# Paired score banks and raised product runs in a hybrid mixer step on one core

## The chip, the cores and the metric

The kernel runs on one core of a Trainium2 chip. The metric is the device time of one execution in microseconds (us), smaller is better. The core has TensorE (PE in the profile; PEld are its weight loads), VectorE (DVE), ScalarE (ACT), GpSimd (POOL) and SyncE (SP, which here issues most of the DMAs). Products of TensorE are written to PSUM, which has eight banks; a bank holds 128 partitions of 512 float32 numbers.

## The reference

One layer of a mixer with three branches over the same input, for 128 context tokens and 512 latent tokens (a grid of 8 rows of 64), width 1024:

```
h     = rmsnorm(x, g_pre) * (1 + scale) + shift      # shift, scale, gate = silu(c) @ w_ada + b_ada
proj  = h @ w_in                                     # 3840 columns
A  8 heads x 64: latent queries see a window of 16 columns of the grid and 256 cached context
   keys in one softmax, with a learned bias; context tokens see the context only
B  4 heads x 64: gated linear recurrence in both directions (HGRN2), state 64 x 64 a head
C  2-D Fourier transform over positions and channels, then a 256 x 256 matrix
out   = concat(A * silu(ga), B * silu(gr), C * silu(gf)) @ w_out
y     = x + gate * rmsnorm(out, g_post)
```

The outputs are y, the context's keys and values, and the final states of the recurrence.

## The kernel before

**Precision and tiling.** Most products run in float32r with both operands split into a high and a low part, and three products are added for each (`mm3`: high x high, low of the input x high of the weights, and the other way round). All 640 tokens stand side by side as columns. The 3840 columns of `w_in` are handled as blocks of 128; a block's result for 320 tokens (half a block) is one bank, filled by 8 x 3 products with 320 columns each (`block`, lines 297 to 312). The weights of a block arrive as 512 KB, are cast to the high part on ScalarE and subtracted on VectorE.

**Streams.** The work is written as generators, which `Order` (lines 39 to 68) merges by estimated times: `start_stream` (modulation vectors, transposed input), `zf_stream` (first two gate blocks, four banks at once), `fill` (all other blocks, in the order of `FILL`), two recurrences, the four attentions of two heads each, the gate vectors of the output, the Fourier branch, and the two halves of the output projection (`out_first`, `out_second`). The merged program order isn't the final one. The kernel is built with `schedule_with_timeline_sim`: a planner keeps a simulated time line, and whenever an engine comes free there, gives it the first instruction in program order whose operands and buffers are ready in the simulation. On the chip every engine then works through its own list in that order. `tc.issue_after` and manual dependencies without a semaphore tie instructions in this planning.

**PSUM.** `PB` (line 105) gives one bank of one of two kinds: tag `b` with five banks, tag `f` with three. `f` holds the half blocks and other sums of the filling streams, three of the four sums of the first gate blocks (line 206) and one of the two tiles in `by_token` (line 343). `b` holds the rest: the transposed input (`px`, `pm`), scores, levels, transposed softmax, weighted values, the recurrence's products and the first output sums. A bank is free again when its last reader is done.

**Products with half the rows.** A head is 64 wide, so two heads share the 128 partitions, head 1 in the upper half of the array's rows, head 0 in the lower. Where a product sums over a head's channels, it takes 64 rows. Three places make such runs and write head 1 and head 0 in turn:
- `level` (lines 431 to 450): for each of seven levels and two head pairs, products `t` x `t` for five units of 128 tokens, four units in one pair of banks and the fifth in another. A float32 product shows as two instructions, so a level has twenty. VectorE merges them under a mask (line 450), ScalarE copies the first level.
- `scores` (lines 641 to 647) from `softmax_latent` (line 669): two calls, six products on the cached keys (`kc`) and six on the latent keys (`tks`), both with the queries `tqs`, into a pair of banks.
- `scores` from `softmax_context` (line 651): six products of 128 columns.

`follow` (line 115) makes each product of such a run come behind the one before it. It doesn't keep other products from between them.

`mod_cols` (lines 192 to 198) makes eight products of 32 output rows each, four side by side in four quarters of the array's columns, sixteen instructions in the profile; `start_stream` calls it twice for each of eight steps, `gate_vectors` once for each of eight blocks. There is no such chain in it.

**Around the softmax.** `softmax_latent` reads the scores on VectorE (maxima, lines 675 and 676) and on ScalarE (the exponentials, lines 679 and 680), then `transposes` (line 705) turns the result with four transposes a head into a bank of `b`, which two casts on ScalarE and two subtractions on VectorE (lines 127 and 128, `pT`) empty. Scores of a tile are issued behind the transposes of the tile two before it (`AHEAD`).

Of the kernel before, what the change touches and what calls it, by code (L numbers as in the profile page):

```python
# [17 lines left out]
P = 128  # L18
# [7 lines left out]
TOKENS = ("ir",)  # L26
WB = {"raw": 2, "hi": 3, "lo": 3, "t": 18, "pe": 2, "o": 4, "cf": 3, "pb": 5, "pf": 3, "s": 8, "m": 4, "row": 2, "tbl": 1, "pT": 8, "vs": 2, "kc": 4}
RAW = ["vs", "pT", "pT", "pT"] * 4
# [43 lines left out]
def mixer_kernel(ctx: ExitStack, tc: tile.TileContext, A, O):  # L72
# [31 lines left out]

    def PB(tag="b"):
        return ps.tile([P, 512], F32, tag=tag, name=nm("pb"), bufs=WB["p" + tag])

# [6 lines left out]

    def follow(chain, ins):

        if chain:
            tc.add_manual_dep(ins, chain[-1].name, mybir.DependencyInfo(mybir.DependencyClass.NoSync,
                                                                        mybir.DependencyReason.DATA), reason="turns")
        chain.append(ins)  # L120
# [70 lines left out]

    def mod_cols(out, w):

        t = od.now
        for k in range(KT):
            o = out[32 * (k % 4):32 * (k % 4) + 32, :]
            mm(o, csil[:, k, :], w[:, k, :], start=(k < 4), stop=(k >= 4))
        od.now = t + 0.45
# [5 lines left out]
    def xcols(i, k):  # L204
        return (xa[i] if k < 5 else xb[i])[:, k % 5 * P:k % 5 * P + P]
    zf_w, zf_acc = [], [[PB("f"), PB("f")], [PB("f"), PB()]]

# [34 lines left out]
    def start_stream():  # L242
        load_x()
        raws, zraw = [], []

        def loads(k):
            for u in range(2):
                raws.append(load_raw(A["wss"][2 * k + u], RAW[2 * k + u]))
            if k < 2:
                zraw.append(load_raw(A["win"][k], "raw"))  # L250

        for k in range(EARLY):
            loads(k)
        scale_x()
        od.now = 11.0
        for k in range(KT):
            if k + EARLY < KT:
                loads(k + EARLY)
            row = sp.tile([P, 256], F32, tag="AC", name=nm("row"), bufs=2)
            pm = PB()  # L260
            for u in range(2):
                mod_cols(pm[:, u * P:(u + 1) * P], raws[2 * k + u])
            yield 0
            ve.tensor_copy(row, pm[:, 0:256])
            yield LAT["row"]

            for u in range(2):
                tr(pm[:, u * P:(u + 1) * P], row[:, u * P:(u + 1) * P])
            pt = S(4)
            ve.reduce_sum(pt, pm[:, 0:256].rearrange("p (u g r) -> p u r g", u=2, r=32)[:, :, 0:2, :], axis=AX.X)  # L270
            ve.tensor_scalar(G[:, k, :], pt[:, 0:2], bss[:, k, 0:1], 1.0, op0=ALU.add, op1=ALU.add)
            ve.tensor_scalar_mul(G[:, k, :], G[:, k, :], gpre[:, k:k + 1])  # L272
            ve.tensor_scalar_add(shift[:, k, :], pt[:, 2:4], bss[:, k, 1:2])
            modulated(k, pm)
            if k < 2:
                zf_w.append(split_w(zraw[k]))
            if k == 1:
                od.set("zw", 0.0)
            yield max(0.0, 13.5 + 2.7 * (k + 1) - od.now)
# [17 lines left out]
    def block(name, use, lo_eng=ve):  # L297

        w = load_w(A["win"][BLOCKS.index(name)], lo_eng)
        for u in range(2):  # L300
            acc = PB("bf"[u] if name == "zb0" else "f")[:, 0:320]
            for k in range(KT):
                if name == "zb0" and u == 0 and f"h{k}" not in od.events:
                    yield f"h{k}"
                mm3(acc, w, k, u, k == 0, k == KT - 1)
                if k % 2 and k < KT - 1:
                    yield 0
            use(acc, u)
            if u == 1:
                od.set(f"block{nb[0]}", 0.0)  # L310
                nb[0] += 1
            yield 0
# [28 lines left out]
    def by_token(src):  # L341

        pt = PB(), PB("f")
        for i in range(5):
            tr(pt[i // 4][:, i % 4 * P:i % 4 * P + P], src[:, i * P:(i + 1) * P])
        return [(slice(4 * j, 4 + j), pt[j][:, 0:(4, 1)[j] * P].rearrange("p (i e) -> p i e", e=P)) for j in range(2)]

    def token_blocks(name, use, tokens, lo_eng=ve):
# [4 lines left out]
        for i0, n in ((0, 2), (2, 2), (4, 1)):  # L353
            acc = PB("f")[:, 0:256 * n].rearrange("p (i e) -> p i e", e=256)
            for i in range(n):
# [58 lines left out]
    def recurrence(p):  # L414
# [16 lines left out]
        def level(KB, QB, li):  # L431
# [3 lines left out]
            for i0, i1 in ((0, 4), (4, 5)):  # L435
                pa = [PB(), PB()]
                t, chain = od.now, []
                for i in range(i0, i1):
                    for hh in (1, 0):
                        ins = mm(pa[hh][:, (i - i0) * P:(i - i0 + 1) * P], KB[RS[hh], i * P:(i + 1) * P],  # L440
                                 QB[RS[hh], i * P:(i + 1) * P])
                        follow(chain, ins)
                od.now = 0.5 * (t + od.now)
# [84 lines left out]

        po = PB(), PB()
        for i in range(5):  # L530
# [106 lines left out]
    def attention(p):  # L637
# [3 lines left out]
        def scores(outs, qt, keys, chain):  # L641

            cols, t = slice(qt * P, (qt + 1) * P), od.now
            for n, (a, b) in enumerate(((0, 0), (0, 1), (1, 0))):
                for hh in (1, 0):
                    follow(chain, mm(outs[hh], qs[a][RS[hh], cols], keys(b)[RS[hh]], start=(n == 0), stop=(n == 2)))
            od.now = 0.5 * (t + od.now)
# [3 lines left out]
        def softmax_context():  # L651
            pss, pes = [PB(), PB()], []
            scores([t[:, 0:P] for t in pss], 0, lambda b: ks[b][:, 0:P], [])
# [15 lines left out]
        def softmax_latent(qt):  # L669
            pss, pes, chain = [PB(), PB()], [], []  # L670
            scores([t[:, 256:512] for t in pss], 1 + qt, lambda b: kcs[b], chain)
# [109 lines left out]
    def fourier_blocks():  # L781
# [7 lines left out]
        for g in range(2):  # L789
            WCS[g] = [T(512, dt=F32R) for _ in range(2)]  # L790
            pw = PB("f")
            for a in range(2):
# [5 lines left out]
    def fourier():  # L798
        Z = [None] * 5
        for i in range(5):  # L800
            pz = PB("f")
            for g in range(2):
# [24 lines left out]
        for u in range(2):  # L827
            pf = PB("f"), PB("f")
            for j in (4, 1, 3, 2, 0):
# [14 lines left out]
    def gate_vectors():  # L844
        selr = cp.tile([P, 2, P], F32R, tag="selr", name="selr")
        gp.tensor_copy(selr, sel)
        for q in range(8):
# [13 lines left out]
            if q % 2 == 0:  # L861
                rows = [sp.tile([P, 256], F32R, tag="AC", name=nm("row"), bufs=2) for _ in range(2)]
            pm, es = PB("f"), slice(q % 2 * P, q % 2 * P + P)
            mod_cols(pm[:, 0:P], w)
            split(pm[:, 0:P], *[t[:, es] for t in rows])
            if q % 2 == 0:
                continue
            yield 1.0
            pg, cs = PB("f"), slice(q % 4 * P - P, q % 4 * P + P)
            for d in range(2):  # L870
# [24 lines left out]
    def out_first():  # L895
# [7 lines left out]
        units = out_units(0, (3,))  # L903
        banks = [PB() for _ in range(4)]
        for n, k in enumerate(kord):
# [3 lines left out]
            for i in range(4):  # L909
                out_mm(banks[i], units[k], i, k, n == 0, n == KT - 1)  # L910
                yield 0
        banks.append(PB("b" if WB["pb"] > 4 else "f"))
        for n, k in enumerate(kord):
# [5 lines left out]
    def out_second():  # L919
# [5 lines left out]
        for i in range(5):  # L925
# [16 lines left out]
            for c in range(0, 512, w):  # L942
                po, cs = PB("f"), slice(c, c + w)
                pieces.append((po, 1, cs))
# [184 lines left out]
```

## Time and profile before

| | |
|---|---|
| runs timed | 3: 436.21, 436.61, 437.71 us |
| median | 436.61 us |
| the profiled execution | 437.11 us |
| its span, first to last instruction | 435.3 us |
| mean granted TensorE clock | 0.996 |
| DMA | 47.62 MB, mean 109 GB/s |

The profile is of one execution. Its span leaves out 1.8 us of that execution's time, ahead of the first and behind the last instruction. In rows of the timeline the columns are: start (us from the span's start), duration, engine, source line, operation, tile written and tiles read, active rows x columns of the array, shape, count of instructions merged into the row, and in brackets the engine's idle time before it with what ended it. Line 113 is the helper `mm` and line 124 the helper `tr`, so products are told apart by tiles: `pb<-hT,hi` and `pb<-hT,lo` are half blocks, `pb<-t,t` with 64 rows are levels, `pb<-kc,tqs` and `pb<-tks,tqs` scores, `pb<-raw,csil` the gate vectors, `pb<-ident,pe` the transposed softmax. A product's duration includes time in the pipeline that it shares with its neighbours; the distance between starts is what it takes from the stream. In rows of the windows the columns are: stretch, its length, then busy time and count for PE, PEld, DVE, ACT and POOL, granted clock, mean busy share of the DMA engines, GB/s.

### The profile page before, as it was taken

The page shows a single profiled execution, that of the slowest core. Times are in us where ns is not written, and L with a number is a line of the kernel's source. Part 1 is how long each engine was busy: PE and PEld are TensorE (multiplying, and loading weights), DVE is VectorE, ACT ScalarE, POOL GpSimd, SP SyncE. Part 2 cuts the span into 40 slices and gives each one's busy share as a digit, 9 for nine tenths or more (in the row PEclk, how much of TensorE's full clock was granted, in tenths as well). Part 3 has the DMA queues.
Part 4 walks back from the last instruction along what each step waited for, and adds up shares of the span by engine and source line. Part 5 has one row for each costly group of instructions (what it writes and reads, how often), then busy time and mean ns, then how long its engine had stood idle before and what let it go on. Part 6 is the DMA issues. An engine that isn't in the chain of part 4 may idle for free.

```text
span 435.3 us, 8309 instructions
## 1 busy us (share of the span) xinstructions
PE 411.3 (94%) x3176; PEld 372.7 (86%) x3176; DVE 303.5 (70%) x866; ACT 205.8 (47%) x546; POOL 7.4 (2%) x23
## 2 busy tenths in 40 slices
PE   0699999999998999999999999999999999999994
PEld 0488899999988998999899889889898988988884
DVE  2775479999986866885597658885768928670174
ACT  6434467565341526654444444753556643350161
POOL 2000000000020100000000000000000000000000
PEclk9999999999999999999999999999999999999998
DMA  7996153211302021122021413245134302481023
GB/s 236 412 407 229 49 158 114 74 45 50 88 20 76 10 62 48 56 97 74 32 68 60 145 50 104 98 147 163 51 119 150 96 0 66 140 291 48 0 105 139
DMA packets 19528, 47.62 MB, mean 109 GB/s; under 512 B 3184, under 2 KB 6912, under 8 KB 19488
## 3 DMA queue, kind: packets, MB, share of 16 engines
q1 hardware_dynamic: 19376, 46.94, 32.0%
q8 instruction: 25, 0.41, 0.4%
q0 software_dynamic: 112, 0.14, 0.3%
q14 instruction: 15, 0.12, 0.1%
HBM read 43.80 MB, written 3.28 MB: 108 GB/s over the span
## 4 chain that ended last, share of the span: by engine, by line
PE 90%; DVE 3%; DMA 3%; ACT 1%; issue 1%; SPq 0%; DVEq 0%; ACTq 0%
PE pb L113 84%; PE pb L124 7%; DMA vs<-wss 2%; DMA txa<-x 1%; DVE AL L450 1%; DVE t L524 1%; DVE AL L487 0%; ACT L679 0%; DVE t L951 0%; ACT pe L680 0%; DVE t L467 0%; DVE t L466 0%; DVE AC L450 0%; DVE t L468 0%; SPq L190 0%
## 5 line engine op out<-in xcount | busy, mean ns | idle before, releaser
L113 PE MATMUL pb<-hT,hi 128*128 128x320 f32 x896 | 208.7, 317 | 2.5 <-DVE vs L128 1.5
L113 PEld LDWEIGHTS pb<-hT,hi 128*128 128x128 f32 x896 | 148.7, 188 | 9.0 <-issue 3.3
L113 PE MATMUL pb<-hT,lo 128*128 128x320 f32 x448 | 139.1, 312 | 0.0
L113 PEld LDWEIGHTS pb<-hT,lo 128*128 128x128 f32 x448 | 84.0, 188 | 1.3 <-DVE G L272 0.2
L128 DVE TENSOR_TENSOR lo<-raw,hi 128x1024 fp32r<-128x1024 f32 x35 | 42.8, 1223 | 18.7 <-ACT hi L127 18.5
L127 ACT CAST hi<-raw 128x1024 fp32r<-128x1024 f32 x35 | 36.8, 1050 | 28.4 <-PE pb L113 17.5
L113 PE MATMUL pb<-t,t 64*128 64x128 f32 (+2 forms) x414 | 42.9, 291 | 0.4 <-DVE AL L450 0.4
L113 PEld LDWEIGHTS pb<-t,t 64*128 64x128 f32 (+1 forms) x414 | 36.0, 188 | 4.7 <-issue 0.7
L127 ACT CAST pT<-pb 128x256 fp32r<-128x256 f32 x64 | 23.5, 373 | 22.3 <-DVE pT L128 11.1
L113 PE MATMUL pb<-hi,mh 128*128 128x512 f32 (+1 forms) x108 | 30.8, 375 | 0.0
L128 DVE TENSOR_TENSOR pT<-pb,pT 128x256 fp32r<-128x256 f32 x64 | 26.5, 419 | 1.7 <-ACT pT L127 1.5
L679 ACT ACTIVATE pe<-pb,s 128x256 f32<-128x256 f32 x32 | 15.3, 478 | 17.5 <-DVE s L678 8.4
L113 PEld LDWEIGHTS pb<-hi,mh 128*128 128x128 f32 x108 | 19.6, 188 | 3.7 <-DVE mh L128 0.3
L113 PE MATMUL pb<-pT,mh 128*128 128x512 f32 (+1 forms) x102 | 21.9, 364 | 0.0
L124 PE MATMUL pb<-ident,pe 128*128 128x128 f32 x136 | 21.0, 274 | 0.5 <-ACT pe L680 0.5
L113 PEld LDWEIGHTS pb<-pT,mh 128*128 128x128 f32 x102 | 17.7, 189 | 3.1
L113 PE MATMUL pb<-lo,mh 128*128 128x512 f32 (+1 forms) x54 | 19.5, 375 | 0.0
L934 ACT ACTIVATE t<-pb 128x512 f32<-128x512 f32 (+1 forms) x11 | 6.1, 552 | 26.9 <-PE pb L113 26.7
L690 DVE TENSOR_TENSOR o<-pb,o 64x512 f32<-64x512 f32 (+1 forms) x16 | 7.8, 486 | 15.5 <-ACT o L689 15.4
L124 PEld LDWEIGHTS pb<-ident,pe 128*128 128x128 f32 x136 | 16.5, 140 | 1.7 <-ACT pe L680 0.7
L450 DVE COPY_PREDICATED AL<-masks,pb 128x512 f32<-128x512 uint32 x24 | 16.6, 742 | 1.7 <-PE pb L113 1.6
L113 PE MATMUL pb<-pT,vs 128*128 128x256 f32 (+1 forms) x96 | 17.0, 320 | 0.0
(205 smaller groups left out, 635.3 us busy)
## 6 DMA issues: line engine op xcount, KB each, us to landing
raw<-win SPq DMA_DIRECT2D x30, 512.0 KB, 3.5
pT<-wss SPq DMA_DIRECT2D x12, 512.0 KB, 10.3
raw<-wg SPq DMA_DIRECT2D x8, 512.0 KB, 3.6
raw<-wout SPq DMA_DIRECT2D x8, 512.0 KB, 3.6
t<-x SPq DMA_DIRECT2D x10, 256.0 KB, 5.4
o_y<-t SPq DMA_DIRECT2D x9, 256.0 KB, 2.2
vs<-wss SPq DMA_DIRECT2D x4, 512.0 KB, 9.5
tbl<-tbl SPq DMA_DIRECT2D x4, 512.0 KB, 3.5
```

The costliest lines, as they stand in the source:

```text
L113: return te.matmul(out, lhsT, rhs, start=start, stop=stop).ins
L124: last_tr[0] = te.transpose(out, src, ident).ins
L127: (sc.copy if hi_eng is None else hi_eng.tensor_copy)(hi, src)
L128: (ve if lo_eng is None else lo_eng).tensor_sub(lo, src, hi.bitcast(F32))
L450: ve.copy_predicated(out, mk.to_broadcast([P, i1 - i0, P]), src)
L524: ve.scalar_tensor_tensor(sall[r, cdst], sall[r, cs], Td[r, ip:ip + 1], pst[r, cdst], op0=ALU.mult, op1=ALU.add)
L679: sc.activation(pe[:, 256:512], ss[:, 256:512], ACT.Exp, bias=m[:, 1:2], accum_out=m[:, 3:4])
L690: ve.tensor_add(out, src[r, :], out)
L934: sc.activation(T(512)[:, cs], po[:, 0:cs.stop - cs.start], ACT.Square, accum_out=ssb[:, j:j + 1])
```

## The change

Banks: tag `b` has four banks and serves everything that asked for `b` or `f` before, except for the pairs. A new tag `s` holds two tiles of two banks each, given out by `PB2`, which returns the two halves. Pairs are the levels, both kinds of scores, the four sums of the first gate blocks, the recurrence's output and four of the first five output sums.

Order: `follow` becomes `run_mm`. It makes the product itself and, for every product of a run but the first, makes it under `tc.high_priority()`, so that the planner takes it ahead of all else that is ready. `mod_cols` uses it too, with a new chain for each call. A level's two parts (four units, one unit) are two chains, as before.

```diff
-WB = {"raw": 2, "hi": 3, "lo": 3, "t": 18, "pe": 2, "o": 4, "cf": 3, "pb": 5, "pf": 3, "s": 8, "m": 4, "row": 2, "tbl": 1, "pT": 8, "vs": 2, "kc": 4}
+WB = {"raw": 2, "hi": 3, "lo": 3, "t": 18, "pe": 2, "o": 4, "cf": 3, "pb": 4, "ps": 2, "s": 8, "m": 4, "row": 2, "tbl": 1, "pT": 8, "vs": 2, "kc": 4}
...
-    def PB(tag="b"):
-        return ps.tile([P, 512], F32, tag=tag, name=nm("pb"), bufs=WB["p" + tag])
+    def PB():
+        return ps.tile([P, 512], F32, tag="b", name=nm("pb"), bufs=WB["pb"])
+
+    def PB2():
+
+        t = ps.tile([P, 2, 512], F32, tag="s", name=nm("ps"), bufs=WB["ps"])
+        return [t[:, j, :] for j in range(2)]
...
-    def follow(chain, ins):
-
+    def run_mm(chain, *args, **kw):
+
+        with tc.high_priority() if chain else ExitStack():
+            ins = mm(*args, **kw)
         if chain:
             tc.add_manual_dep(ins, chain[-1].name, mybir.DependencyInfo(mybir.DependencyClass.NoSync,
                                                                         mybir.DependencyReason.DATA), reason="turns")
...
-    def mod_cols(out, w):
+    def mod_cols(out, w, chain):
 
         t = od.now
         for k in range(KT):
-            o = out[32 * (k % 4):32 * (k % 4) + 32, :]
-            mm(o, csil[:, k, :], w[:, k, :], start=(k < 4), stop=(k >= 4))
+            run_mm(chain, out[32 * (k % 4):32 * (k % 4) + 32, :], csil[:, k, :], w[:, k, :], start=(k < 4), stop=(k >= 4))
...
-    zf_w, zf_acc = [], [[PB("f"), PB("f")], [PB("f"), PB()]]
+    zf_w, zf_acc = [], [PB2(), PB2()]
...
-            acc = PB("bf"[u] if name == "zb0" else "f")[:, 0:320]
+            acc = PB()[:, 0:320]
...
-        pt = PB(), PB("f")
+        pt = PB(), PB()
...
-                pa = [PB(), PB()]
+                pa = PB2()
...
-        po = PB(), PB()
+        po = PB2()
...
-                    follow(chain, mm(outs[hh], qs[a][RS[hh], cols], keys(b)[RS[hh]], start=(n == 0), stop=(n == 2)))
+                    run_mm(chain, outs[hh], qs[a][RS[hh], cols], keys(b)[RS[hh]], start=(n == 0), stop=(n == 2))
...
-            pss, pes = [PB(), PB()], []
+            pss, pes = PB2(), []
...
-            pss, pes, chain = [PB(), PB()], [], []
+            pss, pes, chain = PB2(), [], []
...
-            mod_cols(pm[:, 0:P], w)
+            mod_cols(pm[:, 0:P], w, [])
...
-        banks = [PB() for _ in range(4)]
+        banks = PB2() + PB2()
...
-        banks.append(PB("b" if WB["pb"] > 4 else "f"))
+        banks.append(PB())
```

All other uses of `PB("f")` (Fourier sums, gate vectors, second output half, value blocks) become `PB()`.

More of the change, by code (lines that the diff above doesn't have):

```diff
@@ L261, in start_stream @@
             for u in range(2):
-                mod_cols(pm[:, u * P:(u + 1) * P], raws[2 * k + u])
+                mod_cols(pm[:, u * P:(u + 1) * P], raws[2 * k + u], [])
             yield 0
@@ L353, in token_blocks @@
         for i0, n in ((0, 2), (2, 2), (4, 1)):
-            acc = PB("f")[:, 0:256 * n].rearrange("p (i e) -> p i e", e=256)
+            acc = PB()[:, 0:256 * n].rearrange("p (i e) -> p i e", e=256)
             for i in range(n):
@@ L439, in level @@
                     for hh in (1, 0):
-                        ins = mm(pa[hh][:, (i - i0) * P:(i - i0 + 1) * P], KB[RS[hh], i * P:(i + 1) * P],
-                                 QB[RS[hh], i * P:(i + 1) * P])
-                        follow(chain, ins)
+                        run_mm(chain, pa[hh][:, (i - i0) * P:(i - i0 + 1) * P], KB[RS[hh], i * P:(i + 1) * P],
+                               QB[RS[hh], i * P:(i + 1) * P])
                 od.now = 0.5 * (t + od.now)
@@ L790, in fourier_blocks @@
             WCS[g] = [T(512, dt=F32R) for _ in range(2)]
-            pw = PB("f")
+            pw = PB()
             for a in range(2):
@@ L800, in fourier @@
         for i in range(5):
-            pz = PB("f")
+            pz = PB()
             for g in range(2):
@@ L827, in fourier @@
         for u in range(2):
-            pf = PB("f"), PB("f")
+            pf = PB(), PB()
             for j in (4, 1, 3, 2, 0):
@@ L862, in gate_vectors @@
                 rows = [sp.tile([P, 256], F32R, tag="AC", name=nm("row"), bufs=2) for _ in range(2)]
-            pm, es = PB("f"), slice(q % 2 * P, q % 2 * P + P)
-            mod_cols(pm[:, 0:P], w)
+            pm, es = PB(), slice(q % 2 * P, q % 2 * P + P)
+            mod_cols(pm[:, 0:P], w, [])
             split(pm[:, 0:P], *[t[:, es] for t in rows])
@@ L868, in gate_vectors @@
             yield 1.0
-            pg, cs = PB("f"), slice(q % 4 * P - P, q % 4 * P + P)
+            pg, cs = PB(), slice(q % 4 * P - P, q % 4 * P + P)
             for d in range(2):
@@ L942, in out_second @@
             for c in range(0, 512, w):
-                po, cs = PB("f"), slice(c, c + w)
+                po, cs = PB(), slice(c, c + w)
                 pieces.append((po, 1, cs))
```

## The prediction

> **What bounds the kernel now.** I read the page's busy times and chain first, to see which engine sets the end; then the windows by stage; then TensorE's timeline, because the change touches mostly the order and the banks of its products.
>
> ```profile
> PE 411.3 (94%) x3176; PEld 372.7 (86%) x3176; DVE 303.5 (70%) x866; ACT 205.8 (47%) x546; POOL 7.4 (2%) x23
> PE 90%; DVE 3%; DMA 3%; ACT 1%; issue 1%; SPq 0%; DVEq 0%; ACTq 0%
> 74.00:157.00 83.00, 81.17 (x734) 75.83 (x733) 75.11 (x197) 39.02 (x98) 4.33 (x12) 1.00 0.17 52
> 157.00:345.00 188.00, 187.53 (x1422) 171.24 (x1421) 137.32 (x453) 99.91 (x315) 0.00 (x0) 1.00 0.28 90
> 345.00:390.00 45.00, 45.00 (x263) 40.45 (x262) 27.35 (x58) 18.08 (x35) 0.00 (x0) 1.00 0.36 115
> 390.00:436.00 46.00, 39.38 (x197) 33.41 (x195) 17.57 (x37) 10.95 (x30) 0.00 (x0) 0.95 0.23 84
> ```
>
> TensorE (PE) is 90% of the chain that ended last. In the stage of the recurrence levels (74 to 157 us) and in that of the attentions (157 to 345) it has products in flight nearly without a gap, at a granted clock of 1.00. So the time changes by what TensorE's own stream gets shorter, as long as no new wait appears. VectorE (DVE) is the next engine: 75.11 of 83 us in the level stage, 137.32 of 188 in the attention stage.
>
> A busy TensorE isn't one at its best, so I compare starts. First a score run that is whole (six products on `kc`, six on `tks`), then one that is broken after its first product:
>
> ```profile
> 225.24 0.62 PE L113 MATMUL pb<-kc,tqs 64*128 64x256 f32 x6
> 225.69 0.51 PE L113 MATMUL pb<-tks,tqs 64*128 64x256 f32 x6
> 226.14 0.41 PE L113 MATMUL pb<-hT,lo 128*128 128x320 f32 x1
> ...
> 177.15 0.38 PE L113 MATMUL pb<-kc,tqs 64*128 64x256 f32 x1
> 177.46 0.41 PE L113 MATMUL pb<-hT,hi 128*128 128x320 f32 x1
> 177.71 0.30 PE L113 MATMUL pb<-hT,lo 128*128 128x320 f32 x1
> 177.85 0.45 PE L113 MATMUL pb<-hT,hi 128*128 128x320 f32 x2
> 178.14 0.30 PE L113 MATMUL pb<-hT,lo 128*128 128x320 f32 x1
> 178.38 0.61 PE L113 MATMUL pb<-kc,tqs 64*128 64x256 f32 x5
> 178.72 0.62 PE L113 MATMUL pb<-tks,tqs 64*128 64x256 f32 x6
> 179.27 0.42 PE L113 MATMUL pb<-hT,hi 128*128 128x320 f32 x1
> ```
>
> These products use 64 of the array's rows. The two heads use different halves, so neighbours run side by side: twelve in 226.14 - 225.24 = 0.90 us, 0.15 a pair. One alone takes 177.46 - 177.15 = 0.31. Going between 64-row and full products costs extra on each side: the full product behind it takes 0.25 (177.46 to 177.71) and the last one ahead of the next run 0.24 (178.14 to 178.38), where the rhythm is 0.145 (177.71 to 178.14 for three). That is 0.10 + 0.09 = 0.19 a visit. The eleven that are left take 0.89, as good as the whole twelve.
>
> **The change part by part.** It has two halves: banks (pairs of heads get one tile of two banks, two such tiles; all else shares four banks) and order (products of a run but the first go ahead of everything that is ready). It adds no engine instruction and no DMA; the runs of `mod_cols` get order links, on one engine, without a semaphore.
>
> *Lone first products of latent scores.* There are nine; the first is that at 177.15, the last is
>
> ```profile
> 331.59 0.38 PE L113 MATMUL pb<-kc,tqs 64*128 64x256 f32 x1
> ```
>
> Of the context scores' first products four stand alone; the last of these is
>
> ```profile
> 337.77 0.32 PE L113 MATMUL pb<-tks,tqs 64*128 64x128 f32 x1
> 338.02 0.56 PE L113 MATMUL pb<-hT,hi 128*128 128x320 f32 x2
> ```
>
> Each of the nine costs 0.31 + 0.19 - 0.01 (0.90 against 0.89 for the rest) = 0.49: 9 x 0.49 = 4.4 us. Why they are cut:
>
> ```profile
> 177.31 0.47 ACT L679 ACTIVATE pe<-pb,s 128x256 f32<-128x256 f32 x1 [0.17 <-PE pb L124]
> ```
>
> The exponential of the tile before still reads its bank until 177.78, while the first product has gone at 177.15 into a bank that was free and the second goes at 178.38. In the 5 banks of tag `b` two score pairs (4) and a transpose can't all stand, so a pair gets its banks one after the other. A two-bank tile is given out whole, so the first product can't go before its partner can; the priority keeps other work from between them. Both halves of the change act on this cut, which makes me trust it most.
>
> *Lone first products of context scores.* Four of them: 338.02 - 337.77 = 0.25, plus 0.19, is 0.44. No whole run of six is in the trace; its sixth product is free or costs up to a pair's 0.15, so 0.29 to 0.44. I take 0.40, near the free end, since the twelfth of the latent run was free: 1.6 us.
>
> *Runs cut further in, and level runs.* Three score runs are cut somewhere behind their first product. I price them like the cuts above, at 0.40 (an estimate): 1.2 us. Of the fourteen levels three lose their first product (two instructions), for instance
>
> ```profile
> 77.65 0.49 PE L113 MATMUL pb<-t,t 64*128 64x128 f32 x2
> 78.06 0.56 PE L113 MATMUL pb<-hT,hi 128*128 128x320 f32 x2
> ...
> 78.99 1.38 PE L113 MATMUL pb<-t,t 64*128 64x128 f32 x18
> 80.30 0.41 PE L113 MATMUL pb<-hT,lo 128*128 128x320 f32 x1
> ```
>
> The lone one takes 0.41 by itself, and 0.19 for the visit; the eighteen behind it take 1.31, which I take for a whole level's twenty too. That is 0.60 each: 1.8 us. Runs of 64 rows together: 4.4 + 1.6 + 1.2 + 1.8 = 9.0 us.
>
> A rule that would make this smaller: the Trainium skill, page "TensorE: Matmul & The Clock Gate", section "Measured speedup vs the span model", says that side-by-side tiles take one product's time and some 4 ns for each further tile. By it a lone product costs a pair's 0.15, not 0.31, and the thirteen lone ones together 2.1 us less, an estimate. The row at 177.15 disagrees (0.31), so it is not used.
>
> *Runs of `mod_cols`* (32 columns each, four side by side) are cut the same way in the gate vectors. One run in two pieces, and one whole:
>
> ```profile
> 245.25 0.42 PE L113 MATMUL pb<-raw,csil 128*32 128x128 f32 x6
> 245.60 0.66 PE L124 MATMUL pb<-ident,pe 128*128 128x128 f32 x4
> 246.18 0.62 PE L113 MATMUL pb<-raw,csil 128*32 128x128 f32 x10
> 246.74 0.56 PE L113 MATMUL pb<-hT,hi 128*128 128x320 f32 x2
> ...
> 270.75 0.64 PE L113 MATMUL pb<-raw,csil 128*32 128x128 f32 x16
> 271.33 0.56 PE L113 MATMUL pb<-hT,hi 128*128 128x320 f32 x2
> ```
>
> Whole 0.58; in two 0.35 + 0.56 = 0.91. So a cut costs 0.33, and with the visit's 0.19 (taken from the 64-row rows) 0.52. I count five such cuts in the gate vectors, from that at 245.25 on, and one in the start stage, which would be 3.1; I take 2.5, since some of these pieces stand right beside a score run and share its visit.
>
> *The stall after zf.* TensorE waits for the first gate's activations:
>
> ```profile
> 52.62 0.31 PE L113 MATMUL pb<-hT,lo 128*128 128x320 f32 x1
> 53.95 0.56 PE L113 MATMUL pb<-hT,hi 128*128 128x320 f32 x2 [1.02 <-ACT t L324]
> ```
>
> 1.33 from start to start, 1.2 more than the rhythm: zb0's second half needs a bank of `f`, and all three hold zf's sums. Behind the change it takes one of the shared four, which the transposes of the start have left by then. What is late next is qr0's weights: their cast stands behind the same gate on ScalarE. I keep 0.8 of the 1.2.
>
> *What is lost.* (1) A level's second part (unit 4) begins a new run whose first product isn't raised, so a level may still be cut there: nothing to 14 x 0.60. No cut of this sort is among the three, so near nothing: 1.0. (2) Four shared banks instead of five and three. Accumulators of the blocks, softmax transposes, value tiles and Fourier sums now queue in one line. A case of that kind, where a block waited for a value tile that VectorE was late to read:
>
> ```profile
> 132.21 0.31 PE L113 MATMUL pb<-hT,lo 128*128 128x320 f32 x1
> 133.98 0.39 PE L113 MATMUL pb<-hT,hi 128*128 128x320 f32 x1 [1.46 <-DVE vs L128]
> ```
>
> It is the only wait of this length there. Below nothing: it may go, -1.5. Above: one such wait for each recurrence, head and transposed gate input, some eight, 12 us. I take one more of them, 1.5, as the rows show one.
>
> Sum: 9.0 + 2.5 + 0.8 - 1.0 - 1.5 = 9.8 us off. Against the profiled execution (437.1, of which the span is 435.3 and 1.8 lies around it) that is **427.3 us**; the median of the runs is 436.6, so the profiled one is 0.5 above it. The saving goes through to the end, since TensorE has no pause in which it could be lost: behind the attention stage its own products follow for 45.00 + 39.38 us.
>
> **The rivals.** *The cuts stay in part.* If what splits a run is a wait for an operand (`ks` is only just written when a head's first scores are due), priority can't close it, and other cuts come where runs of equal rank meet. With half of the 11.5 us of cuts left: 437.1 - 5.8 + 2.5 - 0.8 = 433. Against it: most cuts stand right behind the first product, where every operand but the bank is the same. Chance 0.13.
>
> *Nothing on balance.* The bank waits eat the gain, some seven of the 1.5 us kind: about 437. Chance 0.09.
>
> *Slower: the block stream runs out of banks.* Place: 74 to 345 us, where 50 half blocks each need an accumulator. Before, three banks of `f` were out of reach of the softmax transposes; now a pair of transposes can hold two of four, each until VectorE has split it. In this stage that takes:
>
> ```profile
> 176.62 0.60 PE L124 MATMUL pb<-ident,pe 128*128 128x128 f32 x4
> 179.02 0.42 DVE L128 TENSOR_TENSOR pT<-pb,pT 128x256 fp32r<-128x256 f32 x1
> ```
>
> 2.8 us a tile (176.62 to 179.44). With two held so and one block sum being emptied, only the open sum is left, and TensorE stands at its end. The cuts and the stall give 12.7 us, so from 12.7 / 50 = 0.25 us a half block on, all is lost; at 0.4 it is 437.1 - 12.7 + 20 = 444. For it: VectorE has 90% of the level stage. Against: 32 such tiles x 2.8 us are half a bank on average in 188 us, beside one open and one emptied sum: about 2.5 of four. Chance 0.12.
>
> The Trainium skill, page "TensorEngine Tiling (Array Packing)", section "PSUM Bottleneck", says that packing small products speeds TensorE up but not the copies out of PSUM, which may become the bottleneck; that is this rival's direction, and so far the single 1.46 us row speaks for it.
>
> **How the numbers follow.** Forecast (423 to 431): 0.66; half the cuts stay (431 to 435.3): 0.13; nothing (within 0.3%, about what a measurement can tell here): 0.09; slower: 0.12. So faster 0.79, same 0.09, slower 0.12. The range starts at 422, where every term comes in and the wait at 132 goes too (437.1 - 12.7 - 1.5 = 422.9, less run-to-run spread), and ends at 436, beyond the second case.
>
> **What would show it.** Right: the score stretches come in twelves and sixes, none of one; `csil` in sixteens; levels with no stretch of two; no TensorE pause behind zf's last product; the attention stage some 8 us shorter. Wrong: new TensorE idle time whose releaser is VectorE's `pT` or `vs` splits or ScalarE reading a block sum, or a run that still has block products inside it.

## The result, and the profile after

The change made the kernel slower: **485.05 us** against 437.08 us for the kernel before in the same session, a ratio of 1.110 (95% interval 1.104 to 1.116). The prediction was 427.3 us, in a range of 422 to 436.

The first lines are of the page after (busy time, share of the span, instructions) and of its costliest groups (busy us, mean ns of one | idle us of the engine just before them, and what ended most of it).

```profile
span 482.3 us, 8358 instructions
PE 419.9 (87%) x3176; PEld 382.5 (79%) x3176; DVE 305.4 (63%) x866; ACT 205.7 (43%) x546; POOL 7.2 (1%) x23
...
L131 PE MATMUL pb<-ident,pe 128*128 128x128 f32 x136 | 25.1, 312 | 25.6 <-DVE pe L688 21.1
```

The same group on the page before:

```profile
L124 PE MATMUL pb<-ident,pe 128*128 128x128 f32 x136 | 21.0, 274 | 0.5 <-ACT pe L680 0.5
```

The work is the same (3176 products, 866 VectorE instructions), the span is 47.0 us longer, and TensorE is idle 25.6 us ahead of the softmax transposes, where it was idle 0.5 us. What ends that idle time is VectorE, which scales the exponentials (`pe`) that the transposes read. By stage, in the windows after (columns as before):

```profile
74.00:157.00 83.00, 71.42 (x641) 66.78 (x640) 71.08 (x192) 37.13 (x95) 4.11 (x12) 0.94 0.12 39
157.00:345.00 188.00, 164.56 (x1178) 152.43 (x1177) 111.82 (x362) 79.51 (x253) 0.00 (x0) 0.92 0.22 70
345.00:390.00 45.00, 39.60 (x309) 35.28 (x309) 31.83 (x105) 23.97 (x74) 0.00 (x0) 0.92 0.24 82
390.00:436.00 46.00, 46.00 (x269) 41.92 (x268) 25.88 (x50) 16.21 (x26) 0.00 (x0) 1.00 0.30 95
436.00:483.00 47.00, 39.90 (x199) 33.86 (x197) 18.47 (x37) 11.02 (x31) 0.00 (x0) 0.94 0.35 123
```

Between 157 and 345 us, TensorE was busy 187.53 us with 1422 products at a clock of 1.00; now it is busy 164.56 us with 1178 products at 0.92. Two losses stand there at once: pauses, and a lower granted clock. Over the stage VectorE too does less in the same time (111.82 us against 137.32), so its work as a whole isn't the limit; inside the pauses it is what TensorE waits for.

**How one such place looks.** TensorE's timeline after, around 180 us:

```profile
177.86 0.60 PE L131 MATMUL pb<-ident,t 128*128 128x128 f32 x4
179.26 0.63 PE L131 MATMUL pb<-ident,pe 128*128 128x128 f32 x4 [0.80 <-DVE s L686]
180.05 0.63 PE L131 MATMUL pb<-ident,pe 128*128 128x128 f32 x4 [0.16 <-DVE pe L688]
180.61 0.62 PE L118 MATMUL ps<-kc,tqs 64*128 64x256 f32 x6
181.07 0.52 PE L118 MATMUL ps<-tks,tqs 64*128 64x256 f32 x6
182.95 0.63 PE L131 MATMUL pb<-ident,pe 128*128 128x128 f32 x4 [1.37 <-DVE vs L135]
185.40 1.09 PE L131 MATMUL pb<-ident,pe 128*128 128x128 f32 x4 [1.82 <-DVE pe L688]
186.41 1.01 PE L118 MATMUL ps<-kc,tqs 64*128 64x256 f32 x6
187.22 0.84 PE L118 MATMUL ps<-tks,tqs 64*128 64x256 f32 x6
187.99 0.90 PE L118 MATMUL pb<-hT,hi 128*128 128x320 f32 x2
188.69 0.47 PE L118 MATMUL pb<-hT,lo 128*128 128x320 f32 x1
188.96 0.47 PE L118 MATMUL pb<-hT,hi 128*128 128x320 f32 x1
```

The score runs come whole, 6 + 6, as the change wants. But from 177.86 to 187.99 there is no block product (`hT`) at all: TensorE goes from transposes to scores to transposes and waits for VectorE between them: mostly for the exponentials, and at 182.95 for a value tile (`vs`) that VectorE has to read before its bank is free for the transposes. And from 185.40 on everything takes longer: a score run takes 187.99 - 186.41 = 1.58 us where it took 0.90. The windows of this place:

```profile
180.00:183.00 3.00, 1.58 (x17) 1.27 (x18) 2.73 (x13) 2.62 (x11) 0.00 (x0) 1.00 0.39 142
183.00:186.00 3.00, 1.18 (x7) 0.97 (x8) 3.00 (x13) 2.53 (x10) 0.00 (x0) 0.71 0.00 0
186.00:190.00 4.00, 4.00 (x22) 3.45 (x21) 3.82 (x16) 1.86 (x8) 0.00 (x0) 0.50 0.00 0
190.00:193.00 3.00, 3.00 (x20) 2.92 (x19) 0.38 (x3) 0.19 (x1) 0.00 (x0) 0.82 0.00 0
```

TensorE is busy 1.58 and then 1.18 of 3 us, while VectorE is busy 2.73 and 3.00 of them. Then TensorE works for 4 us without a gap at half the full clock. By the clock column (0.71 of 3 us, 0.50 of 4, 0.82 of 3) the half clock lasts 1.7 + 4 + 1.1 = 6.8 us.

**The sum.** Of all starts of neighbouring products that lie over 0.45 us apart, I added what exceeds 0.23 us, the usual distance of the widest products (512 columns). That gives 45.4 us of pauses after (25.3 in the attention stage, 11.9 in the level stage, 6.0 between 345 and 390 us) and 4.2 us before: 41.2 us more. What the cuts gave back is some 12 us at the prediction's own prices (22 stretches of 64 rows fewer, some 9 to 10; five cuts in `csil` runs, 2.6). As 47.0 = 41.2 - 12 + the rest, the rest is some 18 us, and I put it down to the lower clock. This is an estimate; the clock's mean (0.946 over 482.3 us, before 0.996 over 435.3) bounds it at 26.0 - 1.7 = 24 us, part of which falls into the pauses. The clock records of the trace bear it out: ahead of TensorE's last product eight stretches at half clock add up to 47.8 us, and 11.4 us of them are pauses. In the other 36.4 us a block product takes some 0.27 us (188.69 to 188.96) in place of 0.145, so some 17 us are lost there. Before, no such stretch lies ahead of TensorE's last product.

### The profile page after: what moved, and what is told of

It is laid out like the page before. It is cut to its first block, busy times and chain, and to the rows that moved or that the text cites. A ratio compares the mean times of both kernels' runs of the same rounds, so it can differ in the third digit from the quotient of the medians.

```text
span 482.3 us, 8358 instructions
## 1 busy us (share of the span) xinstructions
PE 419.9 (87%) x3176; PEld 382.5 (79%) x3176; DVE 305.4 (63%) x866; ACT 205.7 (43%) x546; POOL 7.2 (1%) x23
## 5 line engine op out<-in xcount | busy, mean ns | idle before, releaser
L118 PE MATMUL pb<-hT,hi 128*128 128x320 f32 x832 | 195.1, 322 | 3.5 <-DVE vs L135 3.5
L131 PE MATMUL pb<-ident,pe 128*128 128x128 f32 x136 | 25.1, 312 | 25.6 <-DVE pe L688 21.1
L118 PE MATMUL ps<-t,t 64*128 64x128 f32 (+1 forms) x312 | 25.4, 287 | 3.8 <-DVE AL L455 2.2
L118 PEld LDWEIGHTS ps<-t,t 64*128 64x128 f32 (+1 forms) x312 | 21.8, 193 | 6.3 <-ACT t L466 2.1
L684 ACT ACTIVATE pe<-ps,s 128x256 f32<-128x256 f32 x32 | 15.3, 478 | 17.6 <-DVE s L683 9.8
L118 PE MATMUL ps<-hT,hi 128*128 128x320 f32 x64 | 16.1, 326 | 1.4 <-DVE hT L244 1.4
L455 DVE COPY_PREDICATED AL<-masks,ps 128x512 f32<-128x512 uint32 x24 | 16.3, 737 | 1.0 <-PE ps L118 1.0
L118 PEld LDWEIGHTS pb<-pT,vs 128*128 128x128 f32 x96 | 14.3, 193 | 3.3 <-ACT pT L134 1.5
L118 PE MATMUL pb<-hi,mh 128*128 128x512 f32 (+1 forms) x60 | 16.7, 361 | 0.0
L118 PE MATMUL pb<-t,t 128*128 128x128 f32 (+1 forms) x102 | 16.2, 309 | 0.0
L685 ACT ACTIVATE pe<-m,s 128x256 f32<-128x256 f32 x32 | 16.1, 503 | 0.0
```

What stands on the lines that cost most here:

```text
L118: return te.matmul(out, lhsT, rhs, start=start, stop=stop).ins
L131: last_tr[0] = te.transpose(out, src, ident).ins
L455: ve.copy_predicated(out, mk.to_broadcast([P, i1 - i0, P]), src)
L684: sc.activation(pe[:, 256:512], ss[:, 256:512], ACT.Exp, bias=m[:, 1:2], accum_out=m[:, 3:4])
L685: sc.activation(pe[:, 0:256], sb, ACT.Exp, bias=m[:, 1:2], accum_out=m[:, 2:3])
```

## The experiments

Three theories were on the table. **A, shortage:** the pairs tie up four banks, and four are too few for the rest. **B, priority:** the raised products push other work back. **C, one line:** the tiles of one tag begin in program order, so that blocks, transposes and value tiles in one tag stand in one line, and whoever is at its head holds up all the others, whether banks are free or not. C came up after the first four runs. All runs stand beside runs of the kernel before on the same chip (436.3 to 437.1 us).

| kernel | us | ratio to before, 95% interval |
|---|---|---|
| the changed kernel | 485.05 | 1.110 (1.104 to 1.116) |
| banks only, no priority | 488.29 | 1.118 (1.114 to 1.121) |
| order only, banks of before | 435.45 | 0.998 (0.996 to 0.999) |
| one pair, six shared banks | 512.89 | 1.174 (1.170 to 1.178) |
| one pair, three shared, three for blocks | 467.05 | 1.071 (1.066 to 1.076) |
| two pairs, two and two | 457.43 | 1.047 (1.045 to 1.048) |
| the same without priority | 463.19 | 1.062 (1.056 to 1.068) |
| before, one tag of eight | 472.74 | 1.082 (1.078 to 1.086) |
| transposes later in program order | 487.98 | 1.118 (1.116 to 1.120) |
| four tiles `pe` | 483.58 | 1.110 (1.105 to 1.114) |
| both of these | 454.6 | 1.040 (1.037 to 1.042) |
| one pair, levels split, three and three | 449.57 | 1.028 (1.023 to 1.033) |
| order only, and the first product later | 431.96 | 0.989 (0.987 to 0.991) |

### The two halves alone

Banks only, from the kernel after:

```diff
-        with tc.high_priority() if chain else ExitStack():
-            ins = mm(*args, **kw)
+        ins = mm(*args, **kw)
```

> The banks of the changed kernel, but no product raised in priority. Theory A (four shared banks starve the block stream, so TensorE stands while VectorE is late): as slow as the changed kernel, 475 to 490 us, with the pause of over 3 us near 146 us still there. Theory B (the raised products pull the attention ahead of the blocks, which leaves nothing to put between its steps): near the kernel before, 425 to 440 us.

Measured 488.29 us: the banks alone bring the whole loss, and B falls. The stretches of 64 rows are 30 (31 in the changed kernel, 53 before), so that the banks by themselves closed the cuts in scores and levels, without priority.

Order only: the kernel before with its five and three banks, `run_mm` in place of `follow`, and `mod_cols` with its chain.

> The priorities of the changed kernel with the banks of the kernel before (five and three, pairs in single banks). Theory A: no new pauses, level runs and mod_cols runs whole, but the lone first products of scores stay, since they come from waiting for the second bank: 431 to 436 us. Theory B: as slow as the changed kernel, 470 to 490 us.

Measured 435.45 us, a ratio of 0.998 (0.996 to 0.999). `csil` comes in sixteens, and the cuts further into the score runs are nearly gone, but the first products still stand alone (twelve runs go on with eleven, four with five), in 54 stretches, and three of the fourteen levels still lose their first product, though the expectation had them whole. So priority can't close a lone first product; the banks can.

### More shared banks

One pair in place of two; the second pairs of the zf sums and of the output's first sums come from the shared tag.

```diff
-"pb": 4, "ps": 2,
+"pb": 6, "ps": 1,
...
-    zf_w, zf_acc = [], [PB2(), PB2()]
+    zf_w, zf_acc = [], [PB2(), [PB(), PB()]]
...
-        banks = PB2() + PB2()
+        banks = PB2() + [PB(), PB()]
```

> The changed kernel with one two-bank tile in place of two, and six shared banks in place of four. Theory A: a good part of the loss comes back, 440 to 465 us, though scores of the next tile now wait for the softmax of this one. If the loss came from the pairs (held longer, given out late) it would be slower still, over 490 us. Theory B: no change, 480 to 490 us.

Measured 512.89 us: with six shared banks it is slower still. A's forecast of 440 to 465 is far off. But the run changes two things at once, and over 490 us was also expected if the pairs themselves are the cause; the single pair has its share, as the next run shows. The timeline of this kernel shows that shared banks weren't what was missing (TensorE, and the VectorE instruction that finishes the next block's weights):

```profile
181.56 1.22 DVE L135 TENSOR_TENSOR lo<-raw,hi 128x1024 fp32r<-128x1024 f32 x1
...
210.35 0.66 PE L131 MATMUL pb<-ident,pe 128*128 128x128 f32 x4
...
217.50 1.09 PE L131 MATMUL pb<-ident,pe 128*128 128x128 f32 x4 [6.50 <-DVE pe L688]
```

TensorE stands still for 6.50 us with the next block's weights ready from 182.78 on (181.56 + 1.22) and, by the last reads of each tile, two of the six banks held. It waits for the exponentials of one softmax tile. The next block product starts at 220.12, behind two groups of transposes and a score run.

Blocks with banks of their own, from the changed kernel: one pair again, three shared banks, and three in a tag `f` that holds what `f` held before.

```diff
-"pb": 4, "ps": 2,
+"pb": 3, "pf": 3, "ps": 1,
...
-            acc = PB()[:, 0:320]
+            acc = PB("f")[:, 0:320]
...
```

> One two-bank tile, three banks for transposes and values, and three that only the block stream and what used tag f before may take; priorities as in the changed kernel. Theory A: whole runs without starved blocks, 424 to 434 us, faster than the kernel before. Theory B: slow, over 465 us.

Measured 467.05 us, so the expected 424 to 434 was missed. Its windows:

```profile
74.00:157.00 83.00, 72.59 (x581) 66.15 (x579) 64.27 (x158) 34.37 (x84) 1.98 (x6) 0.90 0.15 47
157.00:345.00 188.00, 181.31 (x1410) 170.63 (x1411) 130.99 (x410) 87.80 (x275) 1.98 (x6) 0.97 0.26 83
```

With the same single pair, a second line is worth 46 us. In the attention stage TensorE is busy 181.31 us again; most of what is lost is lost in the level stage, where all levels share the one pair: 11.2 us of pauses stand there and 6.8 us in the attention stage (before: 1.9 and 0.6).

### One line, with no bank taken away

For theory C the kernel before gets one single edit: both tags become one tag with all eight banks.

```diff
-        return ps.tile([P, 512], F32, tag=tag, name=nm("pb"), bufs=WB["p" + tag])
+        return ps.tile([P, 512], F32, tag="b", name=nm("pb"), bufs=WB["pb"])
...
-"pb": 5, "pf": 3,
+"pb": 8,
```

> The kernel before with its tags b and f made one tag of eight banks, nothing else. Theory C: slow, 465 to 500 us, with pauses of TensorE in front of the softmax transposes, though no bank was taken away. Theory A: no loss, 425 to 437 us, since every bank is open to all.

Measured 472.74 us. No pairs, no priority, and every bank is there for everybody; 36 us are lost by the common tag alone. The changed kernel lost 12 us more; that part belongs to the pairs and the four banks, and it isn't taken apart by a run of its own. Some of it stands in the level stage, with 11.9 us of pauses in the changed kernel and 3.8 here. The row of the attention stage and one of the waits (us in total, times, longest) show the same picture as the changed kernel:

```profile
157.00:345.00 188.00, 170.32 (x1285) 159.42 (x1283) 118.65 (x389) 83.51 (x271) 0.00 (x0) 0.95 0.24 77
```

```profile
PEld pb L124 <- ACT pT L127: 15.6, 8, 3.2
...
PE pb L124 <- DVE pe L683: 7.6, 5, 2.9
```

The order is made before the chip sees the program. In the compiled list of TensorE's instructions I counted the block products between the starts of neighbouring groups of softmax transposes; the first nine distances, from the first attention on, are

```
before            19  18  12  17  36   9  24  26   0
changed            0   0   0  18   0   6   0  15   9
one tag of eight   0   0   0  18   0   6   0  24   0
```

The tiles' running numbers in that list show that in the changed kernel the 171 tiles of tag `b` begin in program order but for two swaps of neighbours. By this order, the planner fills the time of a softmax with block products only if their tile comes next in its tag. Two tags are two lines, and one can pass the other: in the kernel before, the 92 tiles of `f` begin in program order but for two swaps of neighbours, while across the tags tile 712 begins ahead of tile 660.

Two lines in the changed kernel, its four shared banks split in two and two:

```diff
-"pb": 4, "ps": 2,
+"pb": 2, "pf": 2, "ps": 2,
...
-            acc = PB()[:, 0:320]
+            acc = PB("f")[:, 0:320]
...
```

> The changed kernel, its four shared banks split into two tags of two: f for the block stream and what asked for f before (and the modulation sums of the start), b for the rest. Pairs and priorities stay. Theory C (tiles of one tag begin in program order, so in a shared tag a block's sum stands in line behind transposes that wait for VectorE): the long pauses in front of the softmax transposes go, 422 to 437 us. Theory A (too few banks): not better than the changed kernel, 480 us or more, since the blocks now have two banks in place of four.

Measured 457.43 us, 28 us below the changed kernel with the same four banks. That is the direction of C, but 20 us above its range; A's 480 us or more is out too. The attention stage:

```profile
157.00:345.00 188.00, 179.13 (x1405) 167.15 (x1405) 133.93 (x448) 91.93 (x296) 0.00 (x0) 1.00 0.25 80
```

I sorted the pauses by what stood free in their middle. For this each product and each read in the trace is matched with the compiled lists, which name its bank. In the changed kernel 33.6 of 45.4 us have a free bank in the tag and the next block's weights ready (the line). 10.0 have all four banks held, 7.1 of them between 133 and 150 us, for example this one, behind value tiles that VectorE splits late (the other 1.8 lie at the start, ahead of the first block):

```profile
145.61 0.44 PE L118 MATMUL ps<-t,t 128*128 128x128 f32 x2
149.58 0.87 PE L118 MATMUL pb<-hT,hi 128*128 128x320 f32 x2 [3.53 <-DVE vs L135]
```

With two and two banks it is the other way round: of 28.5 us of pauses 26.9 have both banks of the blocks' tag held. So the line costs more than the shortage, and behind it the shortage is real: two banks are few.

> As the kernel with two tags of two, but no product raised. Pairs alone keep most score runs whole: 1 to 4 us slower than with priorities by the cuts that come back in levels, scores and mod_cols (under 0.6 us each). Theory A: 480 us or more.

The same without priority (the diff of the first experiment): 463.19 us. Priority is worth 5.8 us here, more than the 1 to 4 expected.

### What the head of the line waits for

The transposes 10 us instead of 4 behind their scores in program order:

```diff
-       "prep": 5.0, "sm": 4.0, "pT": 1.6, "mx": 2.0}
+       "prep": 5.0, "sm": 10.0, "pT": 1.6, "mx": 2.0}
```

> The changed kernel with one number changed: the estimate of the softmax's delay, by which its transposes are placed in program order behind the scores, is 10 us in place of 4. Banks, tags and priorities stay. Theory C (a tag is served in program order, so transposes placed too early hold up the blocks behind them): more block products stand ahead of the transposes, a good part of the loss comes back, 445 to 470 us. Theory A (number of banks): no change, 480 to 490 us, or slower, since the attentions end later.

Measured 487.98 us: nothing gained, and my forecast from C was missed. The wait that ends with `pe` got shorter all the same, while the sum of pauses stayed at 42.9 us:

```profile
PE pb L131 <- DVE pe L688: 13.2, 8, 3.3
```

The softmax works with two tiles `pe`, one a head, so the next softmax can't write its exponentials before this one's transposes are through. Four tiles, with two tiles `t` fewer to make room, and the shift besides:

```diff
-"t": 18, "pe": 2,
+"t": 16, "pe": 4,
...
-       "prep": 5.0, "sm": 4.0, "pT": 1.6, "mx": 2.0}
+       "prep": 5.0, "sm": 10.0, "pT": 1.6, "mx": 2.0}
```

> The changed kernel with the softmax's transposes 10 us (not 4) behind their scores in program order, and with four tiles pe in place of two (two tiles t fewer, 16 in place of 18, pay for them). It asks why the same shift with two tiles pe moved nothing (487.98, ratio 1.118). Theory C1: with two tiles pe the second tile's exponentials couldn't begin before the first tile's transposes were done, so the head of the line still waited; with four the VectorE waits ahead of the transposes (13.2 us by the row PE pb L131 <- DVE pe, 21.1 before the shift) fall below 7 and the time falls to 455 to 475. Theory C2: it is the one line itself, whoever stands at its head: the pauses move to other tiles (weighted values, value blocks), and the time stays at 480 to 492. Planned order: still no block product between the transposes of a tile's two heads in most places, so C2 is the likelier by my count.

Measured 454.6 us, at the low end of what C1 gave; C2, which I held likelier, falls. The windows and the group of the transposes:

```profile
74.00:157.00 83.00, 70.62 (x619) 65.87 (x616) 72.30 (x192) 36.92 (x94) 3.97 (x12) 0.88 0.13 38
157.00:345.00 188.00, 184.24 (x1447) 172.30 (x1446) 133.04 (x433) 96.12 (x303) 0.00 (x0) 1.00 0.28 87
```

```profile
L131 PE MATMUL pb<-ident,pe 128*128 128x128 f32 x136 | 20.7, 276 | 1.6 <-DVE pT L135 1.3
```

With the one line unchanged, the idle time ahead of the transposes is 1.6 us in place of 25.6, and the attention stage makes 1447 products at a clock of 1.00, more than the 1422 before the change. The level stage is no better than in the changed kernel (71.42 us busy there): 12.9 of this kernel's 23.4 us of pauses stand in it, so most of the 18 us that it still loses against the kernel before isn't the softmax's. Four tiles without the shift close the square:

> The changed kernel with four tiles pe (and sixteen tiles t) in place of two (and eighteen), and the transposes 4 us behind their scores as in the changed kernel. Together with the shift alone (487.98) and both (454.6) it closes the square. If the shift only helps because more tiles pe let the next softmax begin, and the program order stays what sets the line, four tiles alone change little, since in the planned order the transposes of a tile still follow one another with no block product between (0, 0, 0, 24, as in the changed kernel): 478 to 488. If the tiles pe alone were what the head of the line waited for: 455 to 470.

Measured 483.58 us. Each edit alone leaves the time as it is, both together take 30 us off. In the attention stage the line does little harm as long as its head is ready; here that needs both a place far enough back and a buffer that lets the softmax run ahead. Why neither does anything alone isn't taken apart further: with four tiles alone the wait for `pe` falls to 12.6 us, but the sum of pauses stays at 41.6.

### Looking for a version that beats both

One pair for the scores and the level's large part, single banks for its small part, three shared, three for the blocks:

```diff
-"pb": 4, "ps": 2,
+"pb": 3, "pf": 3, "ps": 1,
...
-                pa = PB2()
+                pa = PB2() if i0 == 0 else [PB(), PB()]
...
```

> One two-bank tile (scores, and the four-unit part of a level), three banks of tag b (transposes, values, the one-unit part of a level), three of tag f for the blocks; priorities as in the changed kernel; second half of block zb0 from b. Theory C, with enough banks in each line: the level stage loses less than in the kernel with one pair for all (which had 467 us), the attention stage has whole runs and no long pauses: 430 to 450 us; below 436 if the levels lose under 8 us against the kernel before. Theory A: 467 us or more, as nothing was added to the banks.

Measured 449.57 us, at the end of the expected range. The attention stage is nearly as good as before the change (second row; 187.53 us busy then), but the level stage (first row) is still short of it, with a single pair for its large parts, and 5.9 us of pauses between 345 and 390 us aren't taken apart:

```profile
74.00:157.00 83.00, 79.25 (x648) 72.90 (x646) 64.68 (x168) 36.38 (x89) 4.01 (x12) 0.92 0.15 47
157.00:345.00 188.00, 186.32 (x1482) 175.37 (x1481) 142.36 (x447) 97.84 (x304) 0.00 (x0) 1.00 0.29 91
```

The last one takes the order-only kernel and plans the first score product of a tile behind the last exponential that reads the tile before; the dependency has no semaphore and holds for the planner alone.

```diff
...
                     run_mm(chain, outs[hh], qs[a][RS[hh], cols], keys(b)[RS[hh]], start=(n == 0), stop=(n == 2))
+                    if first and last_exp[0] is not None:
+                        tc.add_manual_dep(chain[0], last_exp[0].name, mybir.DependencyInfo(mybir.DependencyClass.NoSync,
+                                                                                           mybir.DependencyReason.DATA), reason="behind")
...
-                sc.activation(pe[:, 256:512], ss[:, 256:512], ACT.Exp, bias=m[:, 1:2], accum_out=m[:, 3:4])
+                last_exp[0] = sc.activation(pe[:, 256:512], ss[:, 256:512], ACT.Exp, bias=m[:, 1:2], accum_out=m[:, 3:4]).ins
```

> The kernel before with its banks (five and three) and the raised runs, and besides the first score product of a tile planned behind the last exponential of the tile before it, so that fewer lone first products stand in front of block products (planned: seven runs in the form 1 and 11 or 1 and 5 in place of seventeen, 29 score stretches in place of 37). By the prediction's price, 0.49 us for each lone first, ten fewer give 4.9 us: 430.5 against 435.4 without it, ratio to before 0.986 to 0.990. Rival: the score products come later, so that transposes and weighted values behind them wait, and nothing is left of it: 434 to 440.

Measured **431.96 us**, 0.989 (0.987 to 0.991) of before: 1.1% below the kernel before, clear of the noise, and far below the changed one. In the trace score runs in one piece of twelve are ten (three without the edit), lone score products seven (sixteen). Stretches of 64 rows are 46 in place of 54; eight fewer at the prediction's 0.49 us are 3.9 us, and 435.45 - 431.96 = 3.5 us were measured. The rival didn't come: the stage has no new pause.

```profile
157.00:345.00 188.00, 187.60 (x1448) 173.48 (x1447) 140.63 (x462) 100.14 (x320) 0.00 (x0) 1.00 0.28 91
```

## Why the prediction was wrong

**Right: the cuts and about their price; half right: their cause.** The stretches fell from 53 to 31; levels and gate vectors come whole, as these rows of the timeline after show:

```profile
77.54 1.39 PE L118 MATMUL ps<-t,t 64*128 64x128 f32 x20
...
314.77 0.65 PE L118 MATMUL pb<-raw,csil 128*32 128x128 f32 x16
```

That the lone first products come from the banks and not from a want of priority is confirmed by the two halves alone. But the row that the prediction reads for it (a bank read until 177.78) isn't the second product's bank. That one, by the compiled list, was free from 175.44, and in ten of the thirteen cases the second product's bank was free before the first product began; two pairs and one transpose also fit into five banks. So in these cases it isn't a wait on the chip: if a bank was missing, it was in the planner's simulated time, which the trace doesn't show. The price of 0.49 us is about right: by the last experiment eight stretches fewer gave 3.5 us, 0.44 each. The feared second parts of the levels cut nothing. The first rival, that the cuts stay in part, is out.

**Right: the stall after zf is gone.** TensorE goes from zf's last product to the next block at its rhythm (0.4 us of idle time behind it wait for the low part of the next weights, so the 0.8 kept of 1.2 was a fair size):

```profile
54.30 0.31 PE L118 MATMUL ps<-hT,lo 128*128 128x320 f32 x1
54.45 0.31 PE L118 MATMUL pb<-hT,hi 128*128 128x320 f32 x1
```

**Wrong: the second item of what is lost, "four shared banks instead of five and three".** Its sentence even says that all of these tiles "now queue in one line". But it was priced as a shortage of banks, by the one wait of that kind in the trace before, 1.46 us: one more of them, 1.5 us, at most eight, 12 us. The measured pauses are 41.2 us longer, and 33.6 of the 45.4 us have a free bank and weights that are ready. The prediction's own sign of being wrong was idle time behind VectorE's `pT` or `vs` splits; 3.5 us ahead of blocks did end with `vs`, but of the 25.6 us ahead of the transposes 21.1 ended with `pe`, which holds no bank. The question put to the trace was how many banks are held; the one that mattered was who may pass whom. Tags `b` and `f` were two lines, and the three banks of `f` did more than hold sums: they let blocks begin while the next tile of `b` waited for VectorE. The trace of before hardly shows such a wait (0.5 us ahead of the transposes), since the filling work covered it; the single row was no measure of what is left when the cover is gone.

**Wrong: the step that the saving goes through to the end because TensorE has no pause.** It holds for an unchanged list. The list after has stretches with nothing to do for TensorE but transposes and scores, and they carry a second cost that had no term: the granted clock, at 1.00 in the level and attention stages before, fell to 0.92 to 0.94 from 74 to 390 us.

The Trainium skill, page "TensorE: Matmul & The Clock Gate", section "A second HAM failure mode: psum-queue depth-cycling", describes this: frequent short idle times between groups of products make the clock go back and forth between half and full, and throughput suffers by it. The windows from 180 to 193 us agree (1.58 and 1.18 of 3 us busy, then a clock of 0.50 for 6.8 us).

**The slower rival had the right sign and place, and a mechanism that is the smaller part.** It argued with banks held by transposes until VectorE has split them, gave 444 us, and was set aside since only about 2.5 of four banks are needed on average. The mean hides that all four are held in places, for 10.0 us of the pauses, but it was about right for the rest, and there it was beside the point: eight banks in one line lose 36 us (472.74), and a second line with the same four makes it better (457.43 us with two and two).

The Trainium skill, page "Perfetto Trace Analysis", section "Optimization Strategy", points to the same cause: it reads gaps that recur on the engine that should be saturated as a possible sign that there isn't enough memory for the next tile. Here, by the eight banks in one tag, they came with no bank taken away: of 33.8 us of pauses in that kernel 28.9 have a free bank and weights that are ready.

## What to carry to other kernels

A shared pool of buffers that is given out in program order is a queue: before merging two pools, ask which stream passes which today, and what the head of the merged queue will wait for. A mean count of buffers in use doesn't answer that; the list of one engine's instructions does, by what stands between two steps of the same dependent chain. And where a small planner hint gives part of the wished order (here a first product planned later, 0.989), it is worth trying ahead of any change to the buffers.

## What the runs showed of the hardware

Pauses that are short by themselves can go with a fall of the clock: within the second of two idle times of 1.37 and 1.82 us, with 0.63 us of work between them, the granted clock went to 0.50 and stayed there for 6.8 us. A block product then took 0.27 us from start to start in place of 0.145. Across the kernels, the attention stage (157 to 345 us) ran at 1.00 with TensorE busy 184.24 us or more of 188, at 0.95 with 170.32, and at 0.92 with 164.56. The busy share alone doesn't set it, though: with 179.13 us busy the clock was 1.00, with 181.31 it was 0.97.
